# DeltaNet chunk matrices from decay rows broadcast by DMA, with the sample tokens' state products ahead of them

## The chip, the cores and the metric

The kernel runs on one NeuronCore of a Trainium2 chip. TensorE (PE) multiplies matrices, VectorE (DVE), ScalarE (ACT) and GpSimd (POOL) work on elements, and SyncE (SP) does nothing here but issue most of the DMAs. The metric is the time of one execution on the device in microseconds, as the median of several runs.

## The reference, cut to what matters

One layer of a decoder is run for 256 prompt tokens and for 8 sample streams of 4 tokens each. One branch is a gated DeltaNet with 8 heads of 128 channels, computed in chunks of 64 tokens. What the change touches are the two 64x64 matrices of each chunk, `lower` and `a_intra`, and for the sample tokens the products of keys and queries with the stored state.

```python
gc = jnp.cumsum(g ..., axis=-1)                 # running log decay within the chunk
diff = gc[..., :, None] - gc[..., None, :]
decay = jnp.where(incl, jnp.exp(jnp.where(incl, diff, 0.0)), 0.0)
kb = kc * bc[..., None]
lower = jnp.where(strict, einsum('nbhid,nbhjd->nbhij', kb, kc) * decay, 0.0)
tinv = triangular_solve(eye + lower, eye)
u = tinv @ (vc * bc[..., None])
w = tinv @ (kb * jnp.exp(gc)[..., None])
a_intra = jnp.where(incl, einsum('nbhid,nbhjd->nbhij', qc, kc) * decay, 0.0)
# then per chunk: v_new = u - w @ s;  o = (q*exp(gc)) @ s + a_intra @ v_new;  s = s*exp(g_last) + k' @ v_new
```

## The kernel before, in words

**The main stream.** All 288 tokens (256 prompt, 32 sample) are kept transposed, and every large projection is a stream of weight tiles of 512 KB. SP loads a tile into one of five buffers `raw`, ACT casts it to `wh` (L180), DVE forms the remainder `wl` = `raw` - `wh` (L184), and PE multiplies with both: for each 128x128 block three matmuls of 288 columns (L256 to L258, called main matmuls below), 24 for a tile. `wh` and `wl` have three buffers each, so the cast for a tile waits until PE has read the tile three places before. An item is a run of tiles that fill four PSUM banks, which ACT or DVE then empties.

**The work beside it.** Branches such as the DeltaNet are Python generators that are advanced between tiles at set rates. `gdn(hg)` handles four heads (a group), hg 0 and hg 1 in turn. When the program is built, a scheduler that simulates a timeline fixes the order of instructions on each engine; on the chip each engine takes them strictly in that order. Small tiles come from a pool `U` of 98 slots that is recycled first in, first out, and the generators share four PSUM banks in rotation.

**One group.** A group has nine blocks x: 8 for the sample tokens, 0 to 7 for (head, 128 prompt tokens). Its stages are:

- `nat`: three transposes for each block, the squared norms, `kn` and `bv`; then the scales `s`, `rk`, `nbe`, `kdc` and `qsc`.
- `gram`, nine times (L725 to L743): PE multiplies keys with keys and queries (L725), makes the log decay differences as V . (g*U) (L726), and spreads the column `s` over a block by a transpose of a broadcast (L727). ACT makes g*U (L723) and takes the exponential (L729), POOL masks it (L730), DVE makes `la` in three instructions (L733 twice, L735). For x below 8 the 32x32 diagonal blocks of `la` are gathered into `ltc`.
- `ltc` goes to DRAM (`dlt`, L747) and comes back with another layout (`lb`, L749).
- `gdn_sample`: 16 tiles of stored state are loaded (L894) and multiplied in 128 small matmuls (`kss`, L899).
- The inverse of the 32x32 blocks: 31 steps of two DVE instructions on `X` (L762, L764), interleaved with the main stream's `wl`. The result goes to DRAM (`dx`, L768, L769) and comes back twice in a layout for PE (`dc`, L772).
- For each of the eight prompt blocks POOL spreads `dc` into `dd` (L778), PE multiplies `m1` (L784), ACT copies the result (L785), PE multiplies `ded` (L787) and DVE makes `x1` (L788). Then come the steps along the chunks.

Of the kernel before, what the change touches and what calls it, by code (L numbers as in the profile page):

```python
# [9 lines left out]
F32 = mybir.dt.float32  # L10
F32R = mybir.dt.float32r
AF = mybir.ActivationFunctionType
OP = mybir.AluOpType
# [20 lines left out]
          ("mask0", 36), ("maskt", 50), ("icnt", 60)]  # L34
# [5 lines left out]
def shape_constants():  # L40
    r = np.arange(128)
    t, i = r[:, None], r[None, :]
    same4 = t // 4 == i // 4
    d = {}
# [5 lines left out]
    d["Vb"] = (t > i) & same4  # L50
    d["m32"] = (i // 32 == t // 32 + 1) & ((t // 32) % 2 == 0)
# [37 lines left out]
class Layer:  # L89
# [335 lines left out]
    def beta_alpha(self):  # L425
# [69 lines left out]
        self.beta, self.gl, self.egc, self.esf, self.egl = beta, g, egc, esf, egl  # L495
# [187 lines left out]
    def gdn(self, hg):  # L683
# [3 lines left out]
        gcol = lambda x: self.gl[:, hg * 9 + x:hg * 9 + x + 1]  # L687
# [5 lines left out]
        X9 = [8] + list(range(8))  # L693
        for x in X9:
# [12 lines left out]
            yield  # L707
# [8 lines left out]
        nc.vector.tensor_scalar(qsc, rq, SC, None, op0=OP.mult)  # L716
        yield
        LA = {}
        ltc = pp.tile([128, 8, 32], F32, name="ltc")
        for x in X9:  # L720
            um, vm = (c["Ub"], c["Vb"]) if x == 8 else (c["U"], c["V"])
            ug = self.U(name="ug")
            nc.scalar.activation(ug[:, :128], um, AF.Copy, scale=gcol(x))  # L723
            p = self.ps("gram")
            nc.tensor.matmul(p[:, 0:256], lhsT=kq(x)[:, 0:128], rhs=kq(x)[:, 0:256], start=True, stop=True)  # L725
            nc.tensor.matmul(p[:, 256:384], lhsT=vm, rhs=ug[:, :128], start=True, stop=True)  # L726
            nc.tensor.transpose(p[:, 384:512], s[:, x:x + 1].to_broadcast([128, 128]), c["ident"])  # L727
            dt = ug[:, 128:256]
            nc.scalar.activation(dt, p[:, 256:384], AF.Exp)  # L729
            nc.gpsimd.tensor_tensor(dt, dt, um, op=OP.mult)  # L730
# [5 lines left out]
            self.free(ug)  # L736
# [138 lines left out]
    def gdn_sample(self, hg, G, la, kn, bv, beta, egc, nbe, kdc, qsc):  # L875
# [6 lines left out]
        pk = self.ps("kss")  # L882
        zv = self.kz
        for q in range(2):
            for b in range(8):
                nc.gpsimd.tensor_copy(zv[:, q, b, :, 4 * b:4 * b + 4],
                                      G["kqs"][:, q * 128:q * 128 + 128].rearrange("p (l b t) -> p l b t", l=4, b=8)[:, :, b])
            yield
        for b in range(8):
            st = []  # L890
            for lp in range(2):
                t = self.U(name="st")
                h0 = hg * 4 + lp * 2
                nc.sync.dma_start(t[:, :256].rearrange("p (l d) -> p l d", l=2),  # L894
                                  self.a["state_gdn"][0, b, h0:h0 + 2].rearrange("l k d -> k l d"))
                st.append(t)
            for q in range(2):
                for l in range(4):
                    nc.tensor.matmul(pk[32 * l:32 * l + 32, q * 128:q * 128 + 128], lhsT=zv[:, q, b, l, :],  # L899
                                     rhs=st[l // 2][:, (l % 2) * 128:(l % 2) * 128 + 128],  # L900
                                     start=b == 0 and q == 0, stop=b == 7, tile_position=(0, 32 * l), skip_group_check=True)
            self.free(*st)
            yield
        R = bv[:, 0:128]
        nc.vector.scalar_tensor_tensor(R, pk[:, 0:128], nbe[:, X:X + 1], R, op0=OP.mult, op1=OP.add)
        qs = bv[:, 128:256]
        nc.scalar.activation(qs, pk[:, 128:256], AF.Copy, scale=egc[:, X:X + 1])
# [684 lines left out]
```

## Time and profile before

| | us |
|---|---|
| median of three runs | 2021.07 (2017.93 to 2021.71) |
| profiled execution, its own time | 2021.38 |
| its span, first to last instruction | 2019.2 |
| PE busy | 1991.4, 99% of the span |
| DVE, ACT, POOL busy | 69%, 45%, 8% |
| mean granted TensorE clock | 0.997 of 2.4 GHz |

PE is busy nearly all the time, so what counts is PE's own work and what PE waits for. A row of a timeline gives the start, the duration, the engine and line, and in brackets the idle time of that engine just before and the instruction that ended it. PE's matmuls overlap, so the price of one is the distance from its start to the next start and not its duration.

### The profile page before, as it was taken

What the parts mean: (1) busy time and instruction counts of PE and PEld (TensorE: products, weight loads), DVE (VectorE), ACT (ScalarE), POOL (GpSimd) and SP (SyncE); (2) the same over time, 40 slices, a digit from 0 to 9 for tenths busy, and PEclk for the clock granted to TensorE, in tenths of its full rate; (3) what the DMA queues carried; (4) which work ended last, traced back from release to release, by engine and by line L of the source; (5) the groups of instructions that cost most, each with busy time, mean ns of one, the idle gap of its engine ahead of it and who ended that gap; (6) DMA issues with size and microseconds to landing.
All of it is one profiled execution on the core that took longest, in us unless ns stands there. A gap on an engine that the chain in (4) does not pass through costs nothing. (4 is left out here: it accounts for less than half of the span.)

```text
span 2019.2 us, 38820 instructions
## 1 busy us (share of the span) xinstructions
PE 1991.4 (99%) x15158; PEld 1973.4 (98%) x15158; DVE 1394.2 (69%) x3031; ACT 914.0 (45%) x1489; POOL 164.0 (8%) x315
## 2 busy tenths in 40 slices
PE   8999999999999999999999999999999999999998
PEld 8999999999999999999999999999999999999998
DVE  7969658468888879888774576655666556665554
ACT  6665474354544344333344554444444334333344
POOL 2345203100000030000000000000000000000001
PEclk9999999999999999999999999999999999999999
DMA  8555545758865667876767677888777877777762
GB/s 273 153 150 167 163 146 151 220 157 292 258 199 172 182 192 238 260 248 189 248 229 229 187 231 227 263 278 263 239 260 250 287 247 261 255 258 228 226 197 89
DMA packets 236248, 442.27 MB, mean 219 GB/s; under 512 B 23888, under 2 KB 68128, under 8 KB 234400
## 3 DMA queue, kind: packets, MB, share of 16 engines
q1 hardware_dynamic: 234752, 437.75, 68.8%
q8 instruction: 119, 1.95, 0.4%
q0 software_dynamic: 1168, 1.45, 0.2%
q14 instruction: 65, 0.53, 0.1%
q10 hardware_dynamic: 144, 0.59, 0.1%
HBM read 427.22 MB, written 66.76 MB: 245 GB/s over the span
## 5 line engine op out<-in xcount | busy, mean ns | idle before, releaser
L184 DVE TENSOR_TENSOR wl<-raw,wh 128x1024 fp32r<-128x1024 f32 x585 | 718.8, 1231 | 428.9 <-ACT wh L180 416.1
L180 ACT CAST wh<-raw 128x1024 fp32r<-128x1024 f32 x585 | 612.0, 1050 | 838.4 <-PE m L257 746.9
L256 PE MATMUL m<-hh,wh 128*128 128x288 f32 x1792 | 531.4, 299 | 0.7 <-DVE pad L650 0.5
L257 PE MATMUL m<-hl,wh 128*128 128x288 f32 x1792 | 529.4, 297 | 0.0
L258 PE MATMUL m<-hh,wl 128*128 128x288 f32 x1792 | 521.5, 297 | 0.9 <-DVE wl L184 0.7
L257 PE MATMUL m<-xgl,wh 128*128 128x288 f32 x1408 | 413.3, 295 | 0.2 <-DVE xgl L1411 0.2
L256 PE MATMUL m<-xgh,wh 128*128 128x288 f32 x1408 | 408.6, 296 | 4.3 <-ACT xgh L1407 3.0
L258 PE MATMUL m<-xgh,wl 128*128 128x288 f32 x1408 | 411.9, 296 | 0.8 <-DVE wl L184 0.7
L256 PEld LDWEIGHTS m<-hh,wh 128*128 128x128 f32 x1792 | 337.0, 188 | 1.9 <-DVE pad L650 0.7
L257 PEld LDWEIGHTS m<-hl,wh 128*128 128x128 f32 x1792 | 337.7, 188 | 1.1 <-issue 1.0
L258 PEld LDWEIGHTS m<-hh,wl 128*128 128x128 f32 x1792 | 334.2, 188 | 2.2 <-DVE wl L184 1.3
L256 PEld LDWEIGHTS m<-xgh,wh 128*128 128x128 f32 x1408 | 263.8, 189 | 5.8 <-ACT xgh L1407 3.7
L257 PEld LDWEIGHTS m<-xgl,wh 128*128 128x128 f32 x1408 | 265.0, 188 | 0.7 <-DVE xgl L1411 0.7
L258 PEld LDWEIGHTS m<-xgh,wl 128*128 128x128 f32 x1408 | 264.3, 188 | 1.3 <-DVE wl L184 1.3
L256 PE MATMUL m<-hidh,wh 128*128 128x288 f32 x704 | 207.2, 295 | 0.3 <-ACT y L1477 0.3
L257 PE MATMUL m<-hidl,wh 128*128 128x288 f32 x704 | 207.1, 295 | 0.0
L258 PE MATMUL m<-hidh,wl 128*128 128x288 f32 x704 | 205.9, 295 | 0.5 <-DVE wl L184 0.5
L256 PEld LDWEIGHTS m<-hidh,wh 128*128 128x128 f32 x704 | 132.3, 188 | 0.5 <-ACT y L1477 0.5
L258 PEld LDWEIGHTS m<-hidh,wl 128*128 128x128 f32 x704 | 131.9, 188 | 0.8 <-DVE wl L184 0.8
L257 PEld LDWEIGHTS m<-hidl,wh 128*128 128x128 f32 x704 | 132.3, 188 | 0.0
L1520 POOL TENSOR_TENSOR yo<-y,xr 128x288 f32<-128x288 f32 x7 | 5.3, 798 | 1098.6 <-DVE y L1511 1098.6
L979 DVE SCALAR_TENSOR_TENSOR st<-vb,kdT,st 128x128 f32<-128x128 f32 x256 | 89.6, 350 | 7.1
(385 smaller groups left out, 2626.7 us busy)
## 6 DMA issues: line engine op xcount, KB each, us to landing
raw<-w_in SPq DMA_DIRECT2D x247, 512.0 KB
raw<-w_gu SPq DMA_DIRECT2D x176, 512.0 KB
raw<-w_down SPq DMA_DIRECT2D x88, 512.0 KB
win_sample<-cache_win SPq DMA_DIRECT2D x64, 512.0 KB
kr<-cache_win SPq DMA_DIRECT2D x112, 256.0 KB
vb<-dv SPq DMA_DIRECT2D x32, 512.0 KB
raw<-w_out SPq DMA_DIRECT2D x32, 512.0 KB
win_sample<-cache_win SPq DMA_DIRECT2D x32, 508.0 KB
```

What stands on the lines that cost most here:

```text
L180: i = nc.scalar.copy(wh, raw)
L184: self.last_wl = nc.vector.tensor_tensor(wl, raw, wh.bitcast(F32), op=OP.subtract)
L256: nc.tensor.matmul(out, lhsT=wh[:, c], rhs=xh, start=k == 0, stop=False)
L257: nc.tensor.matmul(out, lhsT=wh[:, c], rhs=xl, start=False, stop=False)
L258: nc.tensor.matmul(out, lhsT=wl[:, c], rhs=xh, start=False, stop=k == nk - 1)
L979: self.paced(nc.vector.scalar_tensor_tensor(s, v[:, j * 4 + i], self.kdT[:, hg, r:r + 1], s, op0=OP.mult, op1=OP.add), "su")
L1520: (nc.vector if how == "v" else nc.gpsimd).tensor_tensor(out[:, d % 2], y, x, op=OP.add)
```

## The change

Three things are changed. (1) The log decays `gc` and the scales `s` are transposed to rows on PE and stored to DRAM (`drw`). For each block one DMA reads a row pair and broadcasts it over 128 partitions (`rw`, 128 KB). DVE takes the difference to the column and clips it against a mask of 0 and -1e30 (`Um`, `Ubm`), ACT takes the exponential in place, POOL multiplies by the row of `s`, and one DVE instruction of 256 columns makes `la`. The products V . (g*U), the broadcast transposes and two DVE instructions go. (2) `kss` and its state loads move from behind the gram stage to ahead of it. The loads start while the `nat` stage runs. (3) `kz` is filled at the start of `gdn`.

```diff
+        self.gc = self.cp.tile([128, 2, 9], F32, name="gc")
...
+        nc.tensor.transpose(pe[:18, 128:256], self.gc.rearrange("p g x -> p (g x)"), c["ident"])
+        gt = self.U(name="gcT")
+        nc.scalar.copy(gt[:18, :128], pe[:18, 128:256])
+        self.drw = self.dr.tile([18, 2, 128], F32, name="drw")
+        nc.sync.dma_start(self.drw[:, 1], gt[:18, :128])
...
         for x in X9:
+            if x in (5, 7):
+                load_states()
...
+        p = self.ps("sT9")
+        nc.tensor.transpose(p[:9, 0:128], s, c["ident"])
+        t = self.U(name="sT9")
+        nc.scalar.copy(t[:9, :128], p[:9, 0:128])
+        nc.sync.dma_start(self.drw[hg * 9:hg * 9 + 9, 0], t[:9, :128])
...
+        def load_row():
+            x = todo.popleft()
+            rw = self.U(name="rw")
+            nc.sync.dma_start(rw[:, 0:256], self.drw[hg * 9 + x].rearrange("q t -> (q t)")[None, :].to_broadcast([128, 256]))
+            rows.append((x, rw))
+        def decays():
+            x, rw = rows.popleft()
+            dt = rw[:, 128:256]
+            nc.vector.scalar_tensor_tensor(dt, dt, gcol(x), c["Ubm"] if x == 8 else c["Um"], op0=OP.subtract, op1=OP.min)
+            nc.scalar.activation(dt, dt, AF.Exp)
+            nc.gpsimd.tensor_tensor(rw[:, 0:128], rw[:, 0:128], dt, op=OP.mult)
+            return rw
+        pk = self.ps("kss")
+        for b in range(8):
+            if todo_s:
+                load_states()
+            st = states.popleft()
...
+                    nc.tensor.matmul(pk[32 * l:32 * l + 32, q * 128:q * 128 + 128], lhsT=self.kz[:, q, b, l, :],
...
+        nc.scalar.activation(qs, pk[:, 128:256], AF.Copy, scale=egc[:, 8:9])
...
         for x in X9:
-            um, vm = (c["Ub"], c["Vb"]) if x == 8 else (c["U"], c["V"])
-            ug = self.U(name="ug")
-            nc.scalar.activation(ug[:, :128], um, AF.Copy, scale=gcol(x))
+            rw = nxt
+            if todo:
+                load_row()
+            nxt = decays() if rows else None
             p = self.ps("gram")
             nc.tensor.matmul(p[:, 0:256], lhsT=kq(x)[:, 0:128], rhs=kq(x)[:, 0:256], start=True, stop=True)
-            nc.tensor.matmul(p[:, 256:384], lhsT=vm, rhs=ug[:, :128], start=True, stop=True)
-            nc.tensor.transpose(p[:, 384:512], s[:, x:x + 1].to_broadcast([128, 128]), c["ident"])
...
-            for q in range(2):
-                nc.vector.scalar_tensor_tensor(la[:, q * 128:q * 128 + 128], p[:, q * 128:q * 128 + 128],
-                                               rk[:, x:x + 1], dt, op0=OP.mult, op1=OP.mult)
-            nc.vector.tensor_tensor(la[:, 0:128], la[:, 0:128], p[:, 384:512], op=OP.mult)
+            nc.vector.scalar_tensor_tensor(la[:, 0:256], p[:, 0:256], rk[:, x:x + 1], rw[:, 0:256],
+                                           op0=OP.mult, op1=OP.mult)
```

**What the order of instructions becomes.** Names carry buffer numbers, and a semaphore's name in brackets tells which engine or DMA queue a row waits for. On PE before, in group 0, the last gram block (x = 7) is followed at once by the state products.

```order
L258 MATMUL m_1961<-hh_103_984,wl_1965 128x288
L725 MATMUL gram_201_1774<-ev_20_158 128x256 [waits DVE_49,Activation_49]
L726 MATMUL gram_201_1774<-ug_200_1772,cc_81 128x128
L727 MATMUL gram_201_1774<-cc_81,s_1556 128x128
L899 MATMUL kss_205_1795<-st_206_1842,kz_107 32x128 [waits DVE_49,DMAHW3_49,Activation_49,Pool_49]
```

On PE of the changed program the state products end just ahead of the first gram block. The fourth block, `gram_203`, stands 18 main matmuls later and waits for ACT.

```order
L781 MATMUL kss_178_1605<-st_190_1728,kz_107 32x128 [waits DMAHW0_49]
L799 MATMUL gram_192_1795<-ev_21_159 128x256
L799 MATMUL gram_195_1804<-ev_13_151 128x256
L799 MATMUL gram_199_1846<-ev_14_152 128x256 [waits Activation_49]
L258 MATMUL m_1965<-hh_82_775,wh_1813 128x288
```

On ACT of the changed program, the copy of the state products that frees their PSUM bank (`bvs_151<-kss_178`, L788) stands behind the exponentials of the first four broadcast rows. `gram_203` takes that bank. In group 1 it stands behind three of them.

```order
L857 ACTIVATE kn_145_1414<-kn_145_1414,kdc_1590 128x128 x2
L750 COPY sT9_175_1598<-sT9_174_1596 9x128 [waits PE_49]
L767 ACT_TABLE_LOAD [waits DMAHW7_49]
L767 ACTIVATE rw_176_1601<-rw_176_1601 128x128 [waits DVE_49]
L767 ACTIVATE rw_177_1603<-rw_177_1603 128x128 [waits DMAHW0_49,DVE_49]
L767 ACTIVATE rw_191_1790<-rw_191_1790 128x128 [waits DMAHW1_49,DVE_49]
L767 ACTIVATE rw_194_1799<-rw_194_1799 128x128 [waits DMAHW2_49,DVE_49]
L788 ACTIVATE bvs_151_1420<-kss_178_1605,egc_1099 128x128 [waits DVE_49]
```

So the fourth gram block, which waited only for `la` and g*U before, now has a DMA store and a DMA load ahead of it. The second place is in group 1, where the inverse ends. On DVE before, the last steps on `X` follow `wl_5003`.

```order
L184 TENSOR_TENSOR wl_5003<-raw_5000,wh_5002 128x1024 [waits DMAHW7_49,PE_49,Activation_49]
L762 TENSOR_TENSOR tm_4307<-lb_3984,X_4306 32x60 [waits DVE_49]
L764 TENSOR_TENSOR X_4306<-X_4306,tm_4307 32x2x30 [waits DVE_49]
L762 TENSOR_TENSOR tm_4307<-lb_3984,X_4306 32x31 [waits DVE_49]
L764 TENSOR_TENSOR X_4306<-X_4306,tm_4307 32x31 [waits DVE_49]
L766 COPY lb_3984<-X_4306 32x1024 [waits DVE_49]
L184 TENSOR_TENSOR wl_5042<-raw_5039,wh_5041 128x1024 [waits DMAHW1_49,PE_49,Activation_49]
```

On DVE of the changed program the same four steps follow `wl_5102`, with the same rows behind them.

```order
L186 TENSOR_TENSOR wl_5102<-raw_5099,wh_5101 128x1024 [waits DMAHW0_49,PE_49,Activation_49]
L829 TENSOR_TENSOR tm_4271<-lb_4146,X_4270 32x60 [waits DVE_49]
L831 TENSOR_TENSOR X_4270<-X_4270,tm_4271 32x2x30 [waits DVE_49]
L829 TENSOR_TENSOR tm_4271<-lb_4146,X_4270 32x31 [waits DVE_49]
L831 TENSOR_TENSOR X_4270<-X_4270,tm_4271 32x31 [waits DVE_49]
L833 COPY lb_4146<-X_4270 32x1024 [waits DVE_49]
L186 TENSOR_TENSOR wl_5149<-raw_5146,wh_5148 128x1024 [waits DMAHW1_49,PE_49,Activation_49]
```

The pattern is the same; what moved is where PE uses its result. On PE before, the first `m1` of group 1 stands inside the tile after next (`wh_5041` is the first tile behind `wh_5002`), and its `ded` 22 main matmuls behind it.

```order
L257 MATMUL m_4866<-hl_127_1235,wh_5041 128x288
L258 MATMUL m_4866<-hh_126_1234,wl_5042 128x288
L784 MATMUL m1_453_4741<-dd_451_4736,e32_452_4739 128x128 [waits Pool_49]
L256 MATMUL m_4866<-hh_129_1270,wh_5041 128x288
L257 MATMUL m_4866<-hl_130_1271,wh_5041 128x288
```

On PE of the changed program the first `m1` and its `ded` stand next to each other at an item's end, ahead of the first matmul with `wh_5101` and `wl_5102`, that is of the very tile whose `wl` stands ahead of the last steps on `X`.

```order
L259 MATMUL m_4856<-hl_137_1369,wh_5050 128x288
L260 MATMUL m_4856<-hh_136_1368,wl_5051 128x288
L851 MATMUL m1_458_4675<-dd_456_4670,e32_457_4673 128x128 [waits Pool_49]
L854 MATMUL ded_459_4678<-dd_456_4670,e32_457_4673 128x128 [waits Activation_49,Pool_49]
L851 MATMUL m1_462_4688<-dd_460_4683,e32_461_4686 128x128
L258 MATMUL m_5222<-hh_82_775,wh_5101 128x288 [waits Activation_49]
```

Before, 91 main matmuls lie between the moment at which PE frees the buffer of the tile ahead of the last steps on `X` and the first `m1`; in the changed program it is 48, two tiles. In group 0 the last step on `X` and the first `m1` stand like this on DVE of the changed program, with the convolution (`cacc`) of the next part between the steps; the first `m1` stands 81 main matmuls behind the release that the cast for `wl_3198` waits for.

```order
L186 TENSOR_TENSOR wl_3198<-raw_3195,wh_3197 128x1024 [waits DMAHW7_49,PE_49,Activation_49]
L669 SCALAR_TENSOR_TENSOR cacc_3117<-pad4_97,sp_82,cacc_3117 128x312 [waits DVE_49]
L661 COPY pad7_103<-m_2787 128x8x4 [waits Activation_49]
L669 SCALAR_TENSOR_TENSOR cacc_3135<-pad5_99,sp_82,cacc_3135 128x312 [waits DVE_49]
L829 TENSOR_TENSOR tm_2093<-lb_1998,X_2092 32x31 [waits DVE_49]
L669 SCALAR_TENSOR_TENSOR cacc_3117<-pad4_97,sp_82,cacc_3117 128x312 [waits DVE_49]
L669 SCALAR_TENSOR_TENSOR cacc_3135<-pad5_99,sp_82,cacc_3135 128x312 [waits DVE_49]
L831 TENSOR_TENSOR X_2092<-X_2092,tm_2093 32x31 [waits DVE_49]
```

Before, these `cacc` rows stood behind the last step on `X`, not among the steps.

## Rows read from the trace of the kernel before

**Rows 1.** Page, busy time (share of the span) and instructions of each engine.
```profile
PE 1991.4 (99%) x15158; PEld 1973.4 (98%) x15158; DVE 1394.2 (69%) x3031; ACT 914.0 (45%) x1489; POOL 164.0 (8%) x315
```

**Rows 2.** What PE waited for: us in total, times, longest us.
```profile
PE kss L899 <- DMA st<-state_gdn: 3.8, 2, 2.4
PE ded L787 <- POOL dd L778: 1.3, 1, 1.3
```

**Rows 3.** PE timeline, gram blocks of group 0: start us, us, engine, line.
```profile
130.35 0.59 PE L725 MATMUL gram<-ev 128*128 128x256 f32 x2
130.78 0.38 PE L726 MATMUL gram<-ug,cc 128*128 128x128 f32 x2
131.12 0.60 PE L725 MATMUL gram<-ev 128*128 128x256 f32 x2
```

**Rows 4.** PE timeline, state products of both groups and main matmuls behind.
```profile
135.79 3.27 PE L899 MATMUL kss<-st,kz 128*32 128x128 f32 x112
140.47 0.64 PE L899 MATMUL kss<-st,kz 128*32 128x128 f32 x16 [1.41 <-DMA st<-state_gdn]
...
318.26 0.65 PE L899 MATMUL kss<-st,kz 128*32 128x128 f32 x16 [2.43 <-DMA st<-state_gdn]
...
319.07 0.29 PE L258 MATMUL m<-hh,wl 128*128 128x288 f32 x1
319.20 0.30 PE L256 MATMUL m<-hh,wh 128*128 128x288 f32 x1
```

**Rows 5.** ACT timeline ahead of the gram stage of group 0.
```profile
120.27 2.45 ACT L790 ACTIVATE kn<-kn,kdc 128x128 f32<-128x128 f32 x8 [0.33 <-DVE kdc L715]
122.62 0.38 ACT L678 COPY ev<-m 128x288 f32<-128x288 f32 x1
```

**Rows 6.** SP timeline, stores to DRAM that a load waits for.
```profile
141.10 0.37 SPq L747 DMA_DIRECT2D dlt<-ltc  x1
...
204.48 0.33 SPq L768 DMA_DIRECT2D dx<-X  x1
...
315.11 0.38 SPq L747 DMA_DIRECT2D dlt<-ltc  x1
```

**Rows 7.** DVE timeline, the first use of the loaded `lb`, both groups.
```profile
146.84 0.18 DVE L762 TENSOR_TENSOR tm<-lb,X 32x31 f32<-32x31 f32 x1 [5.29 <-DMA lb<-dlt]
...
322.66 0.18 DVE L762 TENSOR_TENSOR tm<-lb,X 32x31 f32<-32x31 f32 x1 [3.34 <-DMA lb<-dlt]
```

**Rows 8.** Timelines of ACT, DVE, POOL and PE, group 1, from the cast to `x1`.
```profile
356.95 1.05 ACT L180 CAST wh<-raw 128x1024 fp32r<-128x1024 f32 x1 [2.15 <-PE m L257]
...
359.87 0.18 DVE L764 TENSOR_TENSOR X<-X,tm 32x31 f32<-32x31 f32 x1
...
368.52 6.17 POOL L778 TENSOR_TENSOR dd<-dc,cc 128x128 f32<-128x128 f32 x14 [31.51 <-DMA dc<-dx]
...
369.21 0.39 PE L784 MATMUL m<-dd,e 128*128 128x128 f32 x2
372.35 0.38 PE L787 MATMUL ded<-dd,e 128*128 128x128 f32 x2
...
372.77 0.29 DVE L788 TENSOR_TENSOR x<-dd,ded 128x128 f32<-128x128 f32 x1 [0.48 <-PE ded L787]
```

**Rows 9.** Timelines of DVE and POOL, group 0, around the end of `X`.
```profile
204.27 0.18 DVE L764 TENSOR_TENSOR X<-X,tm 32x31 f32<-32x31 f32 x1
...
210.37 1.44 DVE L658 SCALAR_TENSOR_TENSOR cacc<-pad,sp,cacc 128x312 f32<-128x312 f32 x3
...
212.04 4.00 POOL L778 TENSOR_TENSOR dd<-dc,cc 128x128 f32<-128x128 f32 x6 [1.92 <-DMA dc<-dx]
```

**Rows 10.** PE timeline at the program's start.
```profile
5.32 1.33 PE L256 MATMUL m<-h0h,wh 128*128 128x288 f32 x4 [5.32 <-ACT h0h L384]
9.67 0.38 PE L258 MATMUL m<-h0h,wl 128*128 128x288 f32 x1
```

**Rows 11.** One stretch: busy time by engine, then granted clock, DMA share, GB/s.
```profile
8.00:10.00 2.00, 2.00 (x10) 1.91 (x9) 0.89 (x2) 1.56 (x4) 0.00 (x0) 1.00 1.04 347
```

More of the change, by code (lines that the diff above doesn't have):

```diff
@@ L33 @@
           ("bsel", 32), ("sel1", 32), ("sel0", 128), ("gsel", 16), ("fold", 128),
-          ("mask0", 36), ("maskt", 50), ("icnt", 60)]
+          ("Um", 128), ("Ubm", 128), ("mask0", 36), ("maskt", 50), ("icnt", 60)]
 M_SPEC = [("mp0", 384), ("mp1", 768)]
@@ L50, in shape_constants @@
     d["Vb"] = (t > i) & same4
+    d["Um"] = np.where(t <= i, 0.0, -1e30)
+    d["Ubm"] = np.where((t <= i) & same4, 0.0, -1e30)
     d["m32"] = (i // 32 == t // 32 + 1) & ((t // 32) % 2 == 0)
@@ L494, in beta_alpha @@
                 nc.scalar.activation(dst[:, :, 8:9], v[:, :, 8:9], AF.Exp)
-        self.beta, self.gl, self.egc, self.esf, self.egl = beta, g, egc, esf, egl
+        self.gc = self.cp.tile([128, 2, 9], F32, name="gc")
+        nc.vector.tensor_copy(self.gc[:, :, 0:8], pc[:, 0:18].rearrange("p (g x) -> p g x", g=2)[:, :, 0:8])
+        nc.vector.tensor_copy(self.gc[:, :, 8:9], pc[:, 128:146].rearrange("p (g x) -> p g x", g=2)[:, :, 8:9])
+        self.beta, self.egc, self.esf, self.egl = beta, egc, esf, egl
         self.egls = []
@@ L507, in beta_alpha @@
             self.egls.append(t2)
+        nc.tensor.transpose(pe[:18, 128:256], self.gc.rearrange("p g x -> p (g x)"), c["ident"])
[3 more added lines that the diff above has]
+        nc.sync.dma_start(self.drw[:, 1], gt[:18, :128])
+        self.free(gt)
     def mixer_plan(self):
@@ L686, in gdn @@
         egl = self.egl[:, hg]
-        gcol = lambda x: self.gl[:, hg * 9 + x:hg * 9 + x + 1]
+        gcol = lambda x: self.gc[:, hg, x:x + 1]
         kq = lambda x: G["kqs"] if x == 8 else G["kq"][x // 2][x % 2]
@@ L693, in gdn, with load_states @@
         X9 = [8] + list(range(8))
+        for q in range(2):
+            for b in range(8):
+                nc.gpsimd.tensor_copy(self.kz[:, q, b, :, 4 * b:4 * b + 4],
+                                      G["kqs"][:, q * 128:q * 128 + 128].rearrange("p (l b t) -> p l b t", l=4, b=8)[:, :, b])
+        states, todo_s = deque(), deque(range(8))
+        def load_states():
+            b, st = todo_s.popleft(), []
+            for lp in range(2):
+                t = self.U(name="st")
+                h0 = hg * 4 + lp * 2
+                nc.sync.dma_start(t[:, :256].rearrange("p (l d) -> p l d", l=2),
+                                  self.a["state_gdn"][0, b, h0:h0 + 2].rearrange("l k d -> k l d"))
+                st.append(t)
+            states.append(st)
         for x in X9:
+            if x in (5, 7):
+                load_states()
             vsrc = G["vTs"][:, :128] if x == 8 else G["vT"][x // 2][:, (x % 2) * 128:(x % 2) * 128 + 128]
@@ L716, in gdn @@
         nc.vector.tensor_scalar(qsc, rq, SC, None, op0=OP.mult)
+        p = self.ps("sT9")
[3 more added lines that the diff above has]
+        nc.sync.dma_start(self.drw[hg * 9:hg * 9 + 9, 0], t[:9, :128])
+        self.free(t)
+        rows, todo = deque(), deque(X9)
+        def load_row():
[3 more added lines that the diff above has]
+            rows.append((x, rw))
@@ new lines, in decays @@
+        def decays():
[6 more added lines that the diff above has]
+        load_row()
+        load_row()
+        pk = self.ps("kss")
+        for b in range(8):
+            if todo_s:
+                load_states()
+            st = states.popleft()
+            for q in range(2):
+                for l in range(4):
+                    nc.tensor.matmul(pk[32 * l:32 * l + 32, q * 128:q * 128 + 128], lhsT=self.kz[:, q, b, l, :],
+                                     rhs=st[l // 2][:, (l % 2) * 128:(l % 2) * 128 + 128],
+                                     start=b == 0 and q == 0, stop=b == 7, tile_position=(0, 32 * l), skip_group_check=True)
+            self.free(*st)
+            yield
@@ L717, in gdn @@
+        R, qs = bv[4][:, 0:128], bv[4][:, 128:256]
+        nc.vector.scalar_tensor_tensor(R, pk[:, 0:128], nbe[:, 8:9], R, op0=OP.mult, op1=OP.add)
+        nc.scalar.activation(qs, pk[:, 128:256], AF.Copy, scale=egc[:, 8:9])
         yield
         LA = {}
+        nxt = decays()
         ltc = pp.tile([128, 8, 32], F32, name="ltc")
         for x in X9:
-            um, vm = (c["Ub"], c["Vb"]) if x == 8 else (c["U"], c["V"])
-            ug = self.U(name="ug")
-            nc.scalar.activation(ug[:, :128], um, AF.Copy, scale=gcol(x))
+            rw = nxt
+            if todo:
+                load_row()
+            nxt = decays() if rows else None
@@ L724, in gdn @@
             p = self.ps("gram")
             nc.tensor.matmul(p[:, 0:256], lhsT=kq(x)[:, 0:128], rhs=kq(x)[:, 0:256], start=True, stop=True)
-            nc.tensor.matmul(p[:, 256:384], lhsT=vm, rhs=ug[:, :128], start=True, stop=True)
-            nc.tensor.transpose(p[:, 384:512], s[:, x:x + 1].to_broadcast([128, 128]), c["ident"])
-            dt = ug[:, 128:256]
-            nc.scalar.activation(dt, p[:, 256:384], AF.Exp)
-            nc.gpsimd.tensor_tensor(dt, dt, um, op=OP.mult)
-            la = self.U(name="la")
@@ L737, in gdn @@
+            self.free(rw)
             LA[x] = la
@@ L881, in gdn_sample @@
         nc.gpsimd.tensor_tensor(x1[:, 128:256], la[:, 0:128], c["mS2"], op=OP.mult)
[L882 to L907, printed above, removed]
+        R, qs = bv[:, 0:128], bv[:, 128:256]
         T = self.U(name="ys")
```

1 line of the change is left out of this document (removed).

## The prediction

> **What bounds the kernel now.** I read the page's busy times first. PE is busy 99% of the span [rows 1], so a change counts in two ways only: what PE executes, and what PE waits for. Next come PE's waits by releaser. They are few, and those of the part that is changed are the state products that wait for their states, 3.8 us in two waits, and one `ded` that waits for `dd`, 1.3 us [rows 2]. Then I read PE's timeline at the gram blocks for the price of each matmul, and the timelines of SP, DVE and POOL where a result goes through DRAM. Last I compared the two orders of instructions, since each engine takes its own strictly in order.
>
> A main matmul costs 0.13 us from start to start [rows 4]. The profiled execution took 2021.38 us by its own time, its span plus 2.2 us. The median is 0.3 us less, so a sum against the one holds for the other.
>
> **PE work removed and added.** In a gram block the keys' product takes 130.35 to 130.78, that is 0.43 us, and V . (g*U) with the broadcast transpose 130.78 to 131.12, 0.34 us [rows 3]. There are 18 blocks: 6.1 us go. Three small transposes come (one for `gc`, one for `s` in each group), at a third of 0.34 each: 0.3 us. PE's own work falls by **5.8 us**, bounds 5.3 and 6.1.
>
> **State products moved.** Their two waits, 1.41 and 2.43 us [rows 4], should go: the states are now requested during the `nat` stage, over ten microseconds ahead of their use in both groups. What the move itself costs PE is nothing, the same 128 matmuls stand elsewhere. **3.8 us** gained. The extra loads on SP stand ahead of some weight tiles. By the order, the tightest of these is still requested 109 main matmuls, 14 us, ahead of its use, so I charge nothing. The saved ACT and DVE instructions (the copy g*U, one of three instructions for `la`) lie beside PE and are worth nothing by themselves. Likewise the `wl` that now stands behind nine clips on DVE: in group 0 PE needs it some 50 main matmuls after `sT9`, and that cover is thin but holds.
>
> **Waits for the broadcast rows.** Four round trips through DRAM are in the trace, from the issue of the store to the first use of what was loaded: 141.10 to 146.84, 5.7 us, 315.11 to 322.66, 7.6 us [rows 6, 7], 204.48 to 212.04, 7.6 us [rows 6, 9], and, from the end of `X`, 360.05 to 368.52, 8.5 us [rows 8]. No row shows a broadcast of one 1 KB row over 128 partitions, so I bound it by these: 5.7 to 8.5, and take 7.0. Let P be the time at which PE makes `sT9`. In group 0 ACT must first empty the item that ends there, 0.4, and scale `kn`, 2.45 [rows 5]; with the copy of `sT9`, the store goes out at P + 3.3. The fourth row is three issues of about 0.37 later than the first. With clip, exponential and the copy that frees the bank (1.0 in all), `gram_203` can start at P + 3.3 + 7.0 + 1.1 + 1.0 = P + 12.4. PE arrives after `sT9` 0.1, the state products 3.6 (112 of the 128 take 3.27 [rows 4]), three blocks of 0.43 and 18 main matmuls, at P + 7.4. It waits 5.0 us (3.7 to 6.5). In group 1 no item has to be emptied, most of `kn` is scaled before, and it is the third row: P + 1.6 + 7.0 + 0.75 + 1.0 = P + 10.4, against P + 7.3, 3.0 us (1.7 to 4.6). Together **8.0 us**. The other gram blocks wait for `la`, which by the same steps is ready within a few tenths of their turn.
>
> **The end of the inverse in group 1.** This is the largest term. In both programs the cast for a tile is released by PE, its `wl` follows, and four steps end `X`. In the trace the cast starts at 356.95, and `X` is complete at 360.05, 3.1 later. POOL has `dc` at 368.52, `m1` runs at 369.21, `ded` at 372.35 (its `dd` is the ninth POOL instruction of 0.44, 14 in 6.17), and `x1` starts at 372.77 [rows 8]. Before, 91 main matmuls lay between the release and `m1`, 12.1 us, and nothing waited. Now it is 48, 6.4 us. `ded` can start 15.4 after the release; behind it `x1` and the copy `ev_491` (0.4), whose slot `x1` frees and whose PSUM bank the next item's first matmul takes, add 1.1. PE thus goes on 16.5 after the release and was there at 6.4. Less 0.7 of its own work, that is **9.4 us**. `X` cannot be earlier: its last steps stand behind the `wl` that waits for the release. With a round trip of 5.7 in place of 8.5 it is 6.6, with the DVE chain late by 1.5 it is 10.9.
>
> Behind that wait comes TensorE's clock. At the program's start PE idles 5.32 us, and then 17 main matmuls take 5.32 to 9.67, 0.26 each [rows 10], where later ones take 0.13. That is near the lower of the clock's two levels, 1.2 GHz, though the granted clock of the stretch reads 1.00, which is 2.4 GHz [rows 11]. After the wait of 2.43 us the spacing is 0.13 at once [rows 4]. The new wait has a first piece of some 5 us and a second of 3, so I add **2.0 us** (0 to 2.5). The Trainium skill, TensorE: Matmul & The Clock Gate, section HAM oscillation, says that pauses of some microseconds throw TensorE back to half its clock each time. By that rule the loss would come here too, and not after the state products' waits; the trace agrees for its two cases.
>
> **The end of the inverse in group 0.** Here 81 main matmuls, 10.7 us, lie between release and `m1`, but four `cacc` instructions of 0.48 (1.44 for three [rows 9]) now stand among the last steps. `X` ends 3.1 + 1.9 + 0.2 = 5.2 after the release. The round trip of this group took 7.6 [rows 6, 9], and the other 8.5; the first `dd` adds 0.45. `m1` can start at 13.3 to 14.2, and PE waits **3.2 us** (1 to 4.5), in place of the 1.3 us that `ded` waited for [rows 2]. Later two pairs `m1`, `ded` stand back to back or nearly so, and the first tile after the long wait is cast 14 main matmuls ahead of its use where two instructions of 1.1 must fit: **1.1 us** for both (0 to 2).
>
> **The sum.** 2021.4 - 5.8 - 3.8 - 1.3 + 8.0 + 9.4 + 2.0 + 3.2 + 1.1 = 2034.2 us. All low bounds together give 2021.4 - 11.2 + 5.4 + 6.6 + 0 + 1 + 0 = 2023.2, all high ones 2021.4 - 10.4 + 11.1 + 10.9 + 2.5 + 4.5 + 2 = 2042.0.
>
> **A rule of another price.** The Trainium skill, DMA: Bandwidth & Descriptors, section Anatomy of one DMA, gives a fixed cost of about 2 us for one transfer, most of it the receipt of the write. By it a round trip would be some 4 us, an estimate, where the rows show 5.7 to 8.5; here the rows decide.
>
> **Rivals.** (A) The round trips are short. The rows loaded are a few KB, while the 5.7 to 8.5 us were all taken by transfers of 128 KB beside the weight stream, and a store of 4.6 KB may land sooner. At 4 us, about half of the longest, `gram_203` waits 2.0 and its fellow 0, group 0's `m1` comes in time, the long wait shrinks to 4.9 and the clock stays: 2021.4 - 10.9 + 2.0 + 4.9 + 1.1 = 2018.5, about 2 us below that if the waits in the gram stage vanish as well. It decides for not slower once a round trip is under some 5.5 us. Against it speaks that `dx` and `dc`, which make the largest term, are not changed in size or kind.
>
> (B) The broadcast is slow. 128 partitions read the same 1 KB, nine times in a row. If each such load held the queue for 2 us, the ninth would land 16 us after the first. Nine clips stand ahead of a `wl` on DVE, whose cover would be gone, and each group would lose about 10 us more: 2034 + 20 = 2054. The trace has no such load; the one nearest, `dc`, in pieces of 128 bytes, took no longer than the others.
>
> (C) The work counts and the waits don't: the inverse ends in time because the moved stages let DVE run ahead. Then 2021.4 - 10.9 + 3 (what is left of the row waits) = 2013.5. The order speaks against it, as said of `X`.
>
> **How the numbers follow.** The forecast has 0.68, its own range 2023 to 2042. A has 0.15, B 0.09, C 0.08. Within 0.2%, 4 us, is what a measurement of this kernel can hardly tell from no change. Slower by more than that is above 2025.1: the forecast but its lowest part, 0.66, and B, 0.09: 0.75. Same, 2017.0 to 2025.1: most of A and the rest, 0.14. Faster: C and the low end of A, 0.11. The range of 2018 to 2043 leaves out C, part of A and B.
>
> **What would show it.** In the new profile's waits, `kss` waiting for states should be gone, and `gram` should wait twice for ACT, 3 to 5 us each. The largest waits should be `m1` on POOL and `ded` on POOL at the end of the item in group 1, near 5 and 3 us, followed by an idle before L258 that ACT ends, and some twenty main matmuls at 0.24. PE's busy time should not fall by more than 6. I am wrong if PE passes the first `m1` of group 1 without a wait of 5 us, or if `dd` there starts less than 6 us after the end of `X`.

## The result and the profile after

The changed kernel takes 2033.18 us (median of 4 runs, 2031.2 to 2038.06), the kernel before 2020.48 beside it. The ratio is 1.0058, with a 95% interval of 1.0041 to 1.0075: slower by 12 us, more than the 0.2% that can be told from no change. The profiled execution took 2034.03 us with a span of 2032.2, against 2019.2 before: 13.0 more. The forecast was 2034. Its total was met, but by terms of other sizes, and that is the lesson of this case.

The page's busy line of the changed kernel:

```profile
PE 1991.9 (98%) x15107; PEld 1973.4 (97%) x15107; DVE 1394.7 (69%) x3015; ACT 910.5 (45%) x1474; POOL 168.5 (8%) x315
```

PE has 51 instructions fewer in the record and is busy no less [rows 1]. This looks as if no work had gone. It has, but other matmuls ran at half the clock, as will be seen. Next, what PE waited for in the changed kernel (us in total, times, longest):

```profile
PE m L851 <- POOL dd L845: 7.1, 2, 4.8
PE gram L799 <- ACT bvs L788: 5.8, 2, 3.2
...
PE ded L854 <- POOL dd L845: 2.1, 1, 2.1
...
PE ots L987 <- ACT os L975: 0.8, 1, 0.8
...
PE ded L854 <- ACT e L852: 0.8, 1, 0.8
...
PE m L258 <- ACT ev L1036: 0.6, 2, 0.4
```

The wait for the states has no row any more [rows 2]. In its place stand `gram` twice, `m1` in both groups (4.8 and 2.4) and `ded` once. The gram stage of group 0 on PE, SP, DVE and ACT:

```profile
122.61 0.27 PE L748 MATMUL sT<-cc,s 128*9 128x128 f32 x1
122.81 3.70 PE L781 MATMUL kss<-st,kz 128*32 128x128 f32 x128
126.44 1.56 PE L799 MATMUL gram<-ev 128*128 128x256 f32 x6
...
133.62 0.70 PE L799 MATMUL gram<-ev 128*128 128x256 f32 x2 [3.24 <-ACT bvs L788]
...
124.60 0.30 SPq L751 DMA_DIRECT2D drw<-sT  x1
126.74 4.19 SPq L759 DMA_DIRECT2D rw<-drw  x9
...
130.57 0.35 DVE L766 SCALAR_TENSOR_TENSOR rw<-rw,gc,cc 128x128 f32<-128x128 f32 x1 [7.51 <-DMA rw<-drw]
...
130.61 1.28 ACT L767 ACT_TABLE_LOAD   x1 [6.04 <-DMA rw<-drw]
131.91 0.77 ACT L767 ACTIVATE rw<-rw 128x128 f32<-128x128 f32 x3
132.94 0.31 ACT L767 ACTIVATE rw<-rw 128x128 f32<-128x128 f32 x1 [0.26 <-DVE rw L766]
133.20 0.37 ACT L788 ACTIVATE bvs<-kss,egc 128x128 f32<-128x128 f32 x1
```

The store of `s` is issued at 124.60, the rows are loaded from 126.74 and first used at 130.57: a round trip of 5.97 us. The store is of 4.6 KB, and each load writes 128 KB. On ACT a table load of 1.28 us and four exponentials stand ahead of the copy that frees the bank for `gram_203`. The end of the inverse in group 1, on SP, POOL, ACT and PE:

```profile
374.30 0.33 SPq L835 DMA_DIRECT2D dx<-X  x1
...
381.95 5.77 POOL L845 TENSOR_TENSOR dd<-dc,cc 128x128 f32<-128x128 f32 x16 [30.87 <-DMA dc<-dx]
...
383.24 0.27 ACT L852 COPY e<-m 128x128 f32<-128x128 f32 x1 [4.65 <-PE m L851]
386.43 0.40 ACT L1036 COPY ev<-m 128x288 f32<-128x288 f32 x1 [2.92 <-DVE x L855]
...
382.41 0.79 PE L851 MATMUL m<-dd,e 128*128 128x128 f32 x2 [4.76 <-POOL dd L845]
385.27 0.80 PE L854 MATMUL ded<-dd,e 128*128 128x128 f32 x2 [2.07 <-POOL dd L845]
...
386.88 0.61 PE L258 MATMUL m<-hh,wh 128*128 128x288 f32 x1 [0.38 <-ACT ev L1036]
387.29 0.44 PE L259 MATMUL m<-hl,wh 128*128 128x288 f32 x1
```

It is the chain that was forecast: `dd` 7.7 us behind the end of `X`, `m1`, `ded`, `x1`, the copy `ev`, the next item. PE stands from 377.5 to 386.9 but for its own three products, and what follows runs at 0.24 from start to start (387.29 to 390.89 for 15 of them). Last, stretches of the changed kernel (busy time by engine, then PEclk, DMA share, GB/s) behind each of the four waits:

```profile
134.50:138.00 3.50, 3.50 (x15) 3.10 (x14) 3.50 (x7) 2.85 (x6) 3.50 (x7) 0.56 0.00 0
227.00:230.50 3.50, 3.50 (x17) 3.50 (x16) 0.21 (x1) 1.07 (x2) 3.50 (x11) 0.51 0.62 226
319.00:322.50 3.50, 3.50 (x13) 2.78 (x14) 3.50 (x9) 2.49 (x8) 3.50 (x9) 0.53 0.09 27
380.50:390.50 10.00, 5.64 (x21) 5.05 (x22) 0.29 (x1) 0.83 (x3) 6.64 (x18) 0.51 0.63 166
391.00:395.00 4.00, 3.73 (x30) 3.54 (x29) 0.33 (x2) 0.92 (x4) 0.00 (x0) 1.00 0.37 129
```

The granted clock is 0.5 there, the lower of the two levels (1.2 GHz), and 1.00 a few us later. The kernel before shows 1.00 everywhere between 100 and 450 us.

To add this up, I took the granted clock in slices of half a microsecond over the whole span. What PE lost to the low clock is its busy time in a slice times one minus the clock, over all slices below 0.97. "Work" is busy time less that loss. All are profiled executions, in us:

| kernel | span | PE idle | lost to low clock | work |
|---|---|---|---|---|
| before | 2019.2 | 27.8 | 4.9 | 1986.5 |
| changed | 2032.2 | 40.3 | 12.7 | 1979.2 |
| e1, m1 later | 2029.1 | 38.6 | 9.4 | 1981.1 |
| e2, move only | 2021.4 | 30.5 | 2.7 | 1988.2 |
| e3, rows only | 2027.5 | 37.2 | 10.9 | 1979.4 |
| e5, decay rows early | 2024.9 | 34.3 | 9.0 | 1981.6 |
| e6, the same, old place | 2029.1 | 35.4 | 10.3 | 1983.4 |
| e8, e1 and copy first | 2033.8 | 37.2 | 15.6 | 1981.0 |
| e9, states early | 2014.9 | 24.8 | 4.3 | 1985.8 |
| e11, one buffer less | 2036.1 | 45.7 | 9.7 | 1980.7 |
| e12, states earlier still | 2018.2 | 27.2 | 6.2 | 1984.8 |

The 13.0 us are 12.5 of idling and 7.8 of low clock, less 7.3 of work. They arise between 100 and 450 us, where the stages that were edited run: there PE idles 5.7 us before and 19.2 after, and the low clock costs nothing before and 8.1 after. In every row 2.7 to 7.5 us of the third column lie behind 450 us (4.8 before, 4.6 changed), so smaller differences in it say nothing of an edit.

Each row is one execution only, and not the median one: those of e1, e5 and e6 are the slowest of their kernels, 2.7 to 4.7 us above the median, and that of e9 is the fastest, 3.1 below. Part of the spread goes with the clock: the executions of the changed kernel took 2031.2 to 2038.06 at mean clocks of 0.992 to 0.990, and those of e4, below, 2028.06 at 0.997 to 2039.1 at 0.993. How much they idle is known for the profiled ones alone. e4, e7 and e10 run unused products and have no row.

### The profile page after: what moved, and what is told of

It reads as the page before. It is cut to its first block, busy times and chain, and to the rows that moved or that the text cites. A ratio compares the mean times of both kernels' runs of the same rounds, so it can differ in the third digit from the quotient of the medians.

```text
span 2032.2 us, 38716 instructions
## 1 busy us (share of the span) xinstructions
PE 1991.9 (98%) x15107; PEld 1973.4 (97%) x15107; DVE 1394.7 (69%) x3015; ACT 910.5 (45%) x1474; POOL 168.5 (8%) x315
```

## The experiments

Ratios are to the kernel before, run beside them on the same chip.

**e1: only the distance of `m1` in group 1.**

```
             nc.sync.dma_start(dc[:, q], dx[q].rearrange(...))
-        yield
+        yield 1
```

> The changed kernel with one word more: the step behind the issue of dc's loads pauses for one tile longer. By the order only group 1 moves: its first m1 stands 93 main matmuls behind the release of the last steps of X, where it stood at 48; group 0 and the gram blocks stay. Theory W (the loss is PE waiting for results that went through DRAM, and the low clock behind each wait): the 8.7 us lost at the end of the inverse in group 1 go, and the low clock behind them (17 main matmuls at 0.24 in place of 0.13, 1.9 us): 2033.2 - 10.6 = 2022.6, 1.001 of the kernel before; the gram waits (5.8 us) and group 0's m1 (2.4) stay as they are. Rival Q (the added row and state loads burden the queues all along, so the wait turns up at a later m1 or at a weight tile): above 2029.

2026.26 us, ratio 1.0026 [1.0016, 1.0035]: 6.5 us of the loss went (0.32% of 2021), not 10.6. PE's waits behind 300 us in e1:

```profile
PE gram L799 <- ACT bvs L788: 2.4, 1, 2.4
PE avs L966 <- DVE ys L962: 1.3, 1, 1.3
PE ots L987 <- ACT os L975: 0.8, 1, 0.8
PE ded L854 <- ACT e L852: 0.7, 1, 0.7
```

`m1` waits no more in group 1, and no low clock follows there. Part is given back in small waits that the changed kernel did not have there (`avs`, `ots`, `ded` for the copy: 2.8 together). In this execution `gram_203` of group 0 waited 5.0, against 3.2.

**e2: only the move.** Decays as before; the state products and their loads ahead.

> Only the state products are put ahead; the decays stay as in the kernel before (U scaled, V product, transposed broadcast). First m1 72 main matmuls behind the release in group 0 and 82 in group 1 (before: 70 and 93). Theory W: the two waits for the states go (3.8 us), PE's work stays, no round trip is added: 2020.5 - 3.8 = 2016.7, up to 2018 if the 82 in group 1 leave a wait of about 1 us. Rival Q (the earlier state loads push weight tiles back on SP): 2020 or more, with new waits for wl.

2025.94 us, 1.0019 [1.0010, 1.0027]: slower than before, where 4 us less was expected. Here my theory failed. The states' wait is gone, and others are in its place; PE in e2, 100 to 430 us:

```profile
PE ot L899 <- ACT bv L895: 2.0, 1, 2.0
PE ded L821 <- POOL dd L812: 1.7, 2, 1.5
PE ots L954 <- ACT os L942: 1.7, 1, 1.7
PE m L818 <- POOL dd L812: 1.2, 1, 1.2
PE m L256 <- DVE pad L650: 1.1, 1, 1.1
PE m L256 <- ACT ev L1003: 0.7, 1, 0.7
```

They sum to 8.4 us, where before had 3.8 for the states, 1.3 for `ded` and 0.5 for `pad`; with the smaller ones PE idles 9.7 us there, against 5.7, and the medians differ by 4. The time lies in rival Q's range, but no `wl` wait is new, so its reason is not this one. Every step behind the moved one meets PE at another place, and some short chains that were hidden are so no longer.

**e3: only the rows.** State products at their old place.

> Only the decays come from rows broadcast by DMA; the state products stay behind the gram blocks as in the kernel before. First m1 81 main matmuls behind the release in both groups. Theory W: PE's work falls by 5.8 us, but nothing stands any more between sT9 and the first gram blocks but 18 main matmuls: gram_203 can start 11.0 us after sT9 in group 0 and 10.2 in group 1 (measured in the changed kernel) and PE is there after 3.8: waits of 7.2 and 6.5, with about 1.6 us of low clock behind each; the 3.8 us for the states stay. 2020.5 - 5.8 + 13.7 + 3.3 = 2031.7. Rival M (the rows by themselves are a gain and the moved state products spoil the inverse's timing): 2016 or less.

2029.27 us, 1.0036 [1.0024, 1.0048]: slower, as expected, by 7 us in place of 11. PE in e3, 100 to 430 us:

```profile
PE gram L765 <- DVE la L767: 8.9, 3, 4.4
...
147.03 1.28 PE L932 MATMUL kss<-st,kz 128*32 128x128 f32 x32 [3.02 <-POOL la L822]
...
142.38 1.71 SPq L927 DMA_DIRECT2D st<-state_gdn  x2
```

The gram blocks wait 8.9 and not 13.7. The states' wait stayed in group 0: the row names POOL, but by the trace PE stood waiting for the state load issued at 142.38, which landed at 146.9. In group 1 it is gone. Rival M falls. Neither edit pays by itself.

**e4 and e10: the wait kept, PE kept busy in it.** Unused products into the bank of `m1`; e10 adds 8 into that of `ded`.

```
             p = self.ps("m1")
+            if x == 0:
+                for _ in range((0, 14)[hg]):   # behind the landing of st0, the store of X
+                    self.behind(nc.tensor.matmul(p[:, 128:256], lhsT=c["ident"], rhs=c["U"], start=True, stop=True), st0)
```

> The changed kernel, with 14 unused 128x128 matmuls (0.2 us each, 3 us in all) put into the wait of 4.8 us that PE has ahead of group 1's first m1; they need nothing but the landing of the store of X, and everything else keeps its order. Theory C (the low granted clock behind a wait is the price of PE having idled, and is separate from the wait): m1 starts when it did, the granted clock stays at 1.00 up to m1, and the 17 main matmuls behind the item's start are at 0.13 in place of 0.24: 2033.2 - 2 = 2031, unless the second wait of 2.1 us (ded) throws the clock by itself, then 2033. Rival D (the slow stretch comes from the transfers or the work itself, not from idling): low clock and 0.24 there as before, 2033 to 2036.

> As the run that filled the first wait of group 1's m1 (14 unused matmuls), with 8 more unused matmuls between m1 and ded, which need only the copy of m1. By the order the third m1 moves ahead of the next item. Theory C (low clock follows on PE's idling): no stretch of low clock between 376 and 395 us; the main matmuls behind are at 0.13; beside the run with one fill the span loses 1.4 us, less some tenths for the third m1: about 2029.5. Rival D: a low stretch stays there.

e4 took 2034.19 us, 1.0062 [1.0047, 1.0077], not to be told from the changed kernel; e10 2030.75, 1.0055 [1.0039, 1.0070]. The times alone decide nothing; the profiles do. e4, then e10, stretches as above:

```profile
380.50:385.50 5.00, 1.20 (x8) 0.82 (x8) 0.00 (x0) 0.27 (x1) 3.59 (x11) 1.00 0.66 179
385.50:389.50 4.00, 3.41 (x17) 3.22 (x17) 0.29 (x1) 0.57 (x2) 3.05 (x9) 0.57 0.65 141
```

```profile
382.00:387.00 5.00, 3.19 (x24) 2.64 (x23) 0.00 (x0) 0.43 (x2) 3.77 (x11) 1.00 0.62 185
387.00:391.00 4.00, 3.78 (x29) 3.69 (x29) 0.57 (x2) 1.33 (x5) 2.86 (x8) 1.00 0.70 138
```

With the first wait filled to its last 1.4 us, the clock fell only behind the second, unfilled one (2.4 us on `ded`); with both filled it did not fall at all, though `dd` came no sooner (7.7 us behind the store's issue) and DMA was as busy. e7 and e11, below, leave both waits open and show the same 10 us of low clock there as the changed kernel. So it is PE's idling that costs the clock at this place, and rival D is refuted for it. The loss there went from 3.0 us to 1.4 and to 0. No gain in time can be told from the changed kernel in either run.

**e7: the same for the gram waits.** 12 and 10 unused products ahead of `gram_203` and its fellow.

> The changed kernel with unused 128x128 matmuls (0.2 us each) in front of the two gram blocks that wait for the rows: 12 in group 0 and 10 in group 1. They need nothing that is late. By the order the first m1 of group 0 falls 93 main matmuls behind the release (80 before) as a side effect, and group 1's stays at 48. Theory C (the low clock comes from PE having idled): the wait at gram shrinks to under 1 us in both groups, PE goes on at the same time as before, but at 1.00: the low stretches of 3.5 to 4 us behind the gram waits (134 and 319 us) and behind group 0's m1 (227 us) go, 1.7 us each; the stretch of group 1's m1 stays. 2033.2 - 5.1 - 2.4 = 2025.7. Rival D (low clock from transfers or load): low clock as before, 2031 or more.

2038.17 us, 1.0078 [1.0065, 1.0090]. The experiment missed its aim: the scheduler let the unused products take the place of main matmuls that had stood ahead of `gram_203`. The waits stayed (6.4 in two), low clock behind both, and the added work came on top. It says nothing on the clock at the gram blocks. As a side effect group 0's first `m1` stands later; that `m1` does not wait any more, and the clock stays at 1.00 there.

**e8: e1, with the bank freed first.** The first exponential on ACT is made to follow the copy of q.S.

> As e1 (m1 later by one tile), and the copy of q.S that frees the state products' bank ordered ahead of the first exponentials on ACT, where it stood behind three of them and a table load of 1.28 us. Theory W (the rows are late, whatever ACT's order): gram_203 passes, but the block behind it needs the bank that the first la frees, and that needs the rows: the wait moves by one block and stays 2.5 to 4 us in group 0, 2 to 3 in group 1, and the time is that of e1, 2026. Rival O (ACT's order made the wait): no gram wait, 2026.3 - 7.5 - 2 = 2017.

2035.08 us, 1.0063 [1.0050, 1.0077], 7.5 us above e1 by the ratios. It too missed: the exponentials of the other rows, which the edit did not bind, still stood ahead of the copy, and only the first block's own came later. The gram waits were 6.5, a `ws` of 2.2 came new, and the low clock cost 15.6 in all. Whether ACT's order alone made part of the gram wait this run leaves open; e11 bears on it.

**e5 and e6: the round trip out of the gram stage.** Only the rows of `gc`, in DRAM since the start, are loaded; `s` comes by a transpose per block on PE.

```
-            nc.sync.dma_start(rw[:, 0:256], self.drw[hg * 9 + x]...to_broadcast([128, 256]))
+            nc.sync.dma_start(rw[:, :128], self.drw[hg * 9 + x, 1][None, :].to_broadcast([128, 128]))
...
+            nc.tensor.transpose(p[:, 384:512], s[:, x:x + 1].to_broadcast([128, 128]), c["ident"])
```

> State products ahead, as in the changed kernel, but the round trip leaves the gram stage: only the rows of cumulated decay come by DMA (they are in DRAM since the start and are requested during the nat stage), and s is again broadcast by one transpose for each block on PE (0.17 us); the pause of one tile behind dc's issue is kept. First m1 93 main matmuls behind the release in both groups. PE's work is 18 x 0.17 = 3.1 us less than in the kernel before. Theory W (the loss was the waits for what goes through DRAM, with the low clock behind each): no wait at gram, none at m1, no low clock between 100 and 400 us. Counting work and the states' waits alone 2021.9 - 3.1 - 3.8 - 1.3 = 2013.7; but the move by itself came out 4 us slower than before where 4 less were expected, by small new waits (ots, ot, pad), so I expect 2016 to 2020, 0.997 to 0.999 of the kernel before. Rival S (the moved state products cost 8 us in any order): 2022 or more.

> As e5, but with the state products at their old place behind the gram blocks and without the added pause: one edit of the change, without its round trip. First m1 81 main matmuls behind the release in group 0 and 93 in group 1. Theory W: no gram wait, the waits for the states stay (3.8 us), PE's work falls by 3.1 us: 2021.9 - 3.1 = 2018.8, 0.9985 of the kernel before. Rival L (loads of rows broadcast to 128 partitions are by themselves a burden, for SP's queue or the weight stream): 2022 or more, with new waits for wl.

e5: 2024.05 us, 1.0013 [1.0004, 1.0022]; e6: 2026.78, 1.0024 [1.0013, 1.0034]. Both miss. The wait for rows is gone, and the work fell (last column of the table), but in e5 PE now reached the gram blocks before `s` itself was computed, and in e6 other chains are waited for. PE in e5, then in e6, 100 to 430 us:

```profile
PE gram L793 <- DVE s L762: 5.1, 2, 3.0
```

```profile
PE ys L938 <- DVE X L792: 3.7, 1, 3.7
```

Both times lie in the range of a rival. S, that the moved state products cost 8 us in any order, asks for more than the 4 that e2 shows for the move. L, that loads of broadcast rows burden SP or the weights, finds `wl` waits of 1.3 in e6, in two, where before has none; that is a small part of the 6.5 us that PE idles more there. Neither is refuted. With both round trips of the changed kernel out of PE's way (e1's distance, and no rows behind `sT9`) e5 keeps 1.0013 of its 1.0058; so most of the loss is gone with them, and none of the gain that was sought appears.

**e11: one working buffer less.** `NU = 97` in place of 98.

> The changed kernel with one working buffer less (97 in place of 98) and no other edit. By the order group 1's first m1 now stands 24 main matmuls behind the release, where it stood at 48, and the first three m1 stand together ahead of the next item; group 0's m1 stays at 80. Theory W (the price of the end of the inverse is the distance in PE's order, and that distance is set by which buffer the next item's output gets): the wait at group 1's m1 grows by 24 x 0.133 = 3.2, from 4.8 to 8.0 us, and the time to 2036.4, 1.007 of the kernel before. Rival F (the distance in the order doesn't matter, since the chain starts with PE's progress): wait 4 to 5.5 us, 2033.

2037.55 us, 1.0089 [1.0075, 1.0102]. PE in e11, behind 300 us:

```profile
PE m L851 <- POOL dd L845: 6.7, 1, 6.7
...
PE ded L854 <- POOL dd L845: 2.2, 2, 1.7
...
315.78 0.37 ACT L788 ACTIVATE bvs<-kss,egc 128x128 f32<-128x128 f32 x1 [1.88 <-DVE bvs L787]
319.42 1.28 ACT L767 ACT_TABLE_LOAD   x1 [3.27 <-DMA rw<-drw]
...
322.65 0.40 PE L258 MATMUL m<-hh,wh 128*128 128x288 f32 x1 [2.36 <-ACT ev L1036]
```

At the end of the inverse the waits sum to 8.9, against 4.8 + 2.1 + 0.4 = 7.3 in the changed kernel: 1.6 more, half of the 3.2 expected. PE came 3.2 sooner, but `dd` came sooner as well, 6.6 us behind the end of `X` in place of 7.7. So the distance counts, against rival F, and the trip's length is not fixed. With e1 there are three distances, 93, 48 and 24 main matmuls, for no wait, 7.3 and 8.9 us. The time rose by more than this, about 6 us by the ratios; PE idles 5.4 more in the whole trace, the rest of it in small waits elsewhere. That a buffer count moves `m1` in the order fits the row of the copy `ev`, which waited for `x1`; but no run isolates this.

e11 also bears on e8's question. In its group 1 the copy that frees the bank comes ahead of the exponentials, and no gram block waits; but PE then waits 2.4 us for an `ev` that stands behind the same late rows. The wait moved and did not go.

**e9 and e12: the states requested earlier, nothing moved.**

```
         for x in X9:
+            if x in (5, 6):          # e12: (3, 4, 5, 6)
+                load_states(x - 5)   # e12: x - 3
...
         for b in range(8):
...
+            if b < 6:                # e12: b < 4
+                load_states(b + 2)   # e12: b + 4
+            st = pre.popleft()
```

> The kernel before, with only the loads of the states requested earlier (the first two pairs during the gram blocks, then two steps ahead); the state products and all other work keep their place, and the order of PE is the same to within one main matmul. Theory W: the two waits for the states (1.4 and 2.4 us) go and no other wait comes, since nothing shifts against the inverse: 2021.6 - 3.8 = 2017.8, 0.998 of the kernel before. Rival S (whatever removes these waits brings others of the same size, as in the run with the move alone): 2021 to 2025.

> As e9 (the kernel before, only the states requested earlier), with four pairs requested during the gram blocks in place of two. PE's order is that of the kernel before to within four main matmuls. Theory W: the wait of 1.8 us for the states that e9 still showed in group 1 goes too; 2021.0 - 3.8 = 2017.2, 0.998 of the kernel before. Rival S (each wait removed comes back elsewhere): 1.000, 2020 to 2022, with another wait of 1.5 to 2 us between 100 and 400 us.

e9: 2020.12 us, 0.9996 [0.9988, 1.0005]; e12: 2019.65, 0.9987 [0.9976, 0.9998]. Both fall short of the 0.998 that was expected. In e9 a wait of 1.8 for the states is left. In e12 none is, and PE waits 3.4 at `ws` where e9 has 0.5:

```profile
PE ws L929 <- DVE ys L926: 3.4, 2, 2.3
```

So rival S, that a wait removed comes back elsewhere, holds in part. e12 is the only version ahead of both kernels, by 0.1%, an effect at the edge of what these runs can tell.

## Why the prediction was right in its time, and where its terms were not

- **PE work, -5.8.** Right. The work column has a mean of 1986.3 us for the four kernels with the old decays (before, e2, e9, e12) and 1980.3 for the five with the rows (changed, e1, e3, e8, e11): 6.0 less. The single pair shows 7.3; the column scatters by 1 to 2 us.
- **States' waits, -3.8.** Right: no row is left. That this gain is kept only as long as nothing else shifts was not seen; e2 shows 8.4 us of other waits.
- **Gram waits, 8.0.** Place right, size 5.8; the cause is read from the rows shown, since e7 and e8, which were to isolate it, missed. The round trip was 6.0 us in group 0 and 6.3 in group 1, not 7.0, and `gram_203` began 11.0 after `sT9`, not 12.4, even with a table load that I had not counted. Group 1: 2.6 for 3.0. Rival B's 2 us a load is refuted: nine issues took 4.19, and by the trace the ninth row landed 3.5 us behind the first.
- **Group 1's `m1`, `ded` and next item, 9.4.** Nearly right: PE was there 6.3 us behind the release and went on at 15.7, forecast 6.4 and 16.5, so 8.7 net of its own work. Of this 7.2 are idle; the other 1.5 are mostly its own three products at the low clock, which the table has in its third column. The trip from the end of `X` to `dd` took 7.7, not 8.5. In e1, with the distance, the wait is gone; e11 has the sign and half the size.
- **Group 0's `m1`, 3.2.** 2.4, with `ded`'s wait of 1.3 gone as forecast, but by two errors that offset each other. `dd` began 5.0 us behind the end of `X`, where 7.6 to 8.5 were charged; and the first `dd` is recorded for 3.17 us, where 0.45 was charged (below). With a `dd` of 0.40 `m1` would have been ready before PE came at 223.4. Here the size was luck.

```profile
217.65 0.33 SPq L835 DMA_DIRECT2D dx<-X  x1
...
222.56 7.47 POOL L845 TENSOR_TENSOR dd<-dc,cc 128x128 f32<-128x128 f32 x13 [1.72 <-DMA dc<-dx]
```

- **The clock, 2.0.** This step failed. I argued that waits of 2.4 us leave the clock alone, from the one case in the trace of before [rows 4], and charged the low clock once. It came behind all four waits, 7.8 us more than before. The Trainium skill, TensorE: Matmul & The Clock Gate, section HAM oscillation, says that pauses between bursts throw the clock anew each time; its example has pauses of about 3 to 5 us. Taken as a rule for every pause it would have charged the gram waits as well. The trace agrees for these four, and goes further than the example: 2.38 us at group 0's `m1` was followed by 0.51. The trace of before had the warning too: at 1016.8 us its clock falls to 0.50 behind waits of 0.8 and 0.5, at 1149.9 behind 1.3, 0.6 and 1.6. So the one case of 2.43 was no ground for a rule.
- **Small waits, 1.1.** Too low. Of what was meant, `ded` waited 0.8 for the copy, and the tile behind the long wait none. But `ots` (0.8), `pad` (1.2, before 0.5), `ws` (0.4), `egls` (0.3) and the second `ev` (0.2) came beside it: about 3 us, mostly of chains that the forecast had not looked at.
- **Rivals.** A, the short trip, came true for group 0's inverse (5.0 us, under its limit of 5.5) and was covered up by the long `dd`; the others took 6.0, 6.3 and 7.7. C, that the waits do not count, falls with the time.

The waits were forecast at 16.6 net (8.0 + 9.4 + 3.2 + 1.1 - 3.8 - 1.3) and came to 12.5; the clock at 2.0 and came to 7.8; the work at -5.8 and came to -7.3. Charging 4.1 too much for the waits and taking 1.5 too little off for the work offset a shortfall of 5.8 in the clock. That the total came out at 2034 is in part luck; the sign is not, since the waits alone outweigh the work that goes.

## What to carry to other kernels

On a static order, moving work saves what the move removes and then pays for every chain whose cover it shifts: take away a wait by an earlier request before you move its consumer (e12, which lost nothing, against e2), and count main matmuls between release and use for every hop through DRAM behind the edit. Price an idle engine twice, once for the wait and once for the slower stretch behind it. Judge such an edit by idle time, low-clock loss and work apart, since PE's busy time alone hid 6 us of saved work here.

## What the runs showed of the hardware that was not expected

- Behind each of the waits of 2.4 to 4.8 us in the changed kernel the granted clock fell to 0.5, for about 3.5 us each time and for 10 behind the last pair, at 1.7 to 3.0 us of lost PE time. Waits of 2 to 3 us went either way: that of 2.43 before was not followed by low clock [rows 4], nor were the 2.4 at `gram` of group 1 in e1 and the longer one of 3.0 at `gram` in e5, while 2.38 at `m1` of group 0 was. What decides between these is open.
- A round trip through DRAM, from the issue of the store to the first use of the load, took 4.9 and 7.7 us for the same 128 KB in groups 0 and 1, and 6.0 and 6.3 where the store was of 4.6 KB. So size explains little of it.
- One POOL instruction was far longer than its like. The 32 `dd` of the changed kernel (ns min, median, max), and DVE beside the long one, group 0's first, which starts at 222.56:

```profile
L845 POOL TENSOR_TENSOR dd<-dc,cc x32: 390/400/3170, 222.6 to 387.3; 128x128 f32<-128x128 f32 x32
...
223.13 2.34 DVE L186 TENSOR_TENSOR wl<-raw,wh 128x1024 fp32r<-128x1024 f32 x2
```

It ends at 225.73, just behind the second of these two `wl`. In all 14 traces the 243 `dd` that ran while DVE was idle took 388 to 403 ns, and every one above 1100 ns lay mostly beside a busy DVE; the first `dd` of group 0 took 3.0 to 3.2 us in e1, e4, e8, e10 and e11 too. So it goes with DVE's work beside it. That DVE holds POOL up is not shown: no run took DVE away from it with all else equal.
